# Banded attention scores: the keys' low parts stored on both 64-partition halves

## The chip, the core and the metric

The kernel runs on one core of a Trainium2 chip. The metric is the device time of one execution in microseconds (us); the median of several runs counts. The engines are named as in the profile: PE is TensorE (matmul), PEld its weight loads, DVE is VectorE, ACT is ScalarE, POOL is GpSimd, SP is SyncE, which issues the DMAs.

## What is computed

Two layers of a transformer trunk over 1024 tokens of width 1024, in float32. Each layer has a mixer, a cross attention to 256 memory tokens and an MLP. The mixer of layer 0 is a recurrent one; that of layer 1, the only place that the change touches, is attention in a sliding window of 128 keys, with 16 query heads of size 64, 4 key heads and a sink per head. Cut to what matters:

```
q = rotary(q.reshape(B, S, SW_HEADS, SW_HD), positions).reshape(B, S, SW_KV_HEADS, SW_GROUP, SW_HD)
k = rotary(k.reshape(B, S, SW_KV_HEADS, SW_HD), positions)
...
    def block(j):
        ...
        s = jnp.einsum('blkgd,bckd->bkglc', qb, kb).astype(jnp.float32) * scale
        s = jnp.where(valid, s, -jnp.inf)
        m = jnp.maximum(jnp.max(s, axis=-1), sink)
        p = jnp.exp(s - m[..., None])
        den = jnp.sum(p, axis=-1) + jnp.exp(sink - m)
        ob = jnp.einsum('bkglc,bckd->blkgd', p, vb.astype(jnp.float32))
        ob = ob / jnp.moveaxis(den, -1, 1)[..., None]
```

Block j has 128 queries; its keys are those of blocks j - 1 and j, and `valid` keeps the last 128 positions of each query. The sum of `s` runs over the 64 features d of a head.

## The kernel before, in words

**Precision.** Every float32 operand x of a matmul is split into a high part h, rounded to the type that PE multiplies fast, and a low part l = x - h. A product x y is made of h h, h l and l h. In most of the kernel these are three matmuls (`mm3`). In the banded attention the three are folded into two, since a head has only 64 features and PE has 128 rows: the stationary operand `qT` holds a query head's high part on one 64-partition half and its low part on the other, and the keys' high part stands on both halves (`K1`). One matmul over 128 rows then gives (q_high + q_low) k_high. The second matmul gives q_high k_low and takes 64 rows only: `ql[hp]`, the half with the query's high part, against `K2`, in which the low parts of two key heads share a tile, one on each half.

**Tiling.** `mixer1` is called for each half of the tokens (512, four tiles of 128). It first makes keys and values for the four tiles (`proj_tok`, `rope`, `keys`, `stage`), then the queries in two column blocks `s`; for each tile and pair of key heads `queries` splits the rotated queries and `attend` runs for one token tile `t` and one key head `g`. So `attend` runs 4 x 4 = 16 times in each half. In `stage2` each run multiplies 4 query heads with the keys: for `t` > 0 the two blocks of keys are one operand of 256 columns, so 8 matmuls; for the first tile of half 0 it is 8 matmuls of 128 columns, and for the first tile of half 1, whose earlier keys are kept in `kprev`, 16 of 128 columns. In all 192 matmuls of 256 columns and 96 of 128, half of them over 64 rows, in strict alternation with those over 128.

**After the scores** ACT copies one half of the columns to `p`, DVE merges the other half in (`copy_predicated`), DVE takes the maximum, ACT the exponentials, POOL normalises and masks, PE transposes `p` back (`stage3`) and multiplies with the values (`stage4`).

**Order.** Matmuls are issued in the order of emission (`ordered("pe", ...)`). Emission follows a nominal clock: `pe(us)` advances it, `defer(d, fn)` puts a step off by d nominal microseconds, and the constants `Q1` to `Q3`, `A1` to `A3`, `B1` to `B3` say how far. A score stage counts as 1.0 us on it (`pe(1.0)`). The order on DVE, ACT and POOL follows from the same emission through a scheduler; each of these engines works strictly in its order. The tiles of the mixer come from one pool of 35 buffers (`X`).

Of the kernel before, what the change touches and what calls it, by code (L numbers as in the profile page):

```python
# [59 lines left out]
def trunk(ctx: ExitStack, tc, a, out, stop=99):  # L60
# [6 lines left out]
    def ordered(key, ins):  # L67
        """Issue the instructions of one key in the order of emission."""
        if key in last_of:
            tc.add_manual_dep(  # L70
                ins.ins,
                last_of[key],
                mybir.DependencyInfo(mybir.DependencyClass.NoSync, mybir.DependencyReason.DATA),
                reason="order",
            )
        last_of[key] = ins.ins.name
        return ins
# [28 lines left out]
    # The order of emission: work that waits for other engines is put off by some  # L106
    # microseconds of the tensor engine's work; a filler's pieces go in between.
# [18 lines left out]
    # The filler: groups (load, start, parts); loads run one group ahead of the starts,  # L126
    # and these one group ahead of the parts.
# [9 lines left out]
    def fill(begin=True):  # L137
        """One piece of the filler; False when there is none left."""
        while True:
            if begin and len(parts) < 2 + 1 and (todo or loaded):  # L140
                load_ahead(1)
                g = loaded.pop(0)
                c = g[1]()
                parts.extend(g[2])
                load_ahead(la[0])
                if c == 0.0:
                    continue
            elif parts:
                c = parts.pop(0)()
            else:  # L150
                return False
            clock[0] += c
            due()
            return True
# [13 lines left out]
    def in_steps(gen, n, d):  # L168
        """Emit n instructions of gen every d microseconds."""

        def step():
            for _ in range(n):
                if next(gen, step) is step:
                    return
            defer(d, step)

        step()
# [36 lines left out]
    def table(**kw):  # L214
        """An activation with a table function, in the order of emission."""
        return ordered("table", act(**kw))
# [4 lines left out]
    # ---------------------------------------------------------------- constants  # L221
# [17 lines left out]
    def columns(rows, n):  # L239
        """[n rows of P] -> [P, n]."""  # L240
        ps = T()
        transpose(out=ps[:, 0:n], in_=rows[0:n], identity=ident[0:n, 0:n])
        t = cp.tile([P, n], F32, name=nm("col"))
        vec.tensor_copy(t, ps[:, 0:n])
        return t
# [6 lines left out]
    # ---------------------------------------------------------------- helpers  # L252
    def rsqrt(ss, n):
        """1 / sqrt(sum(ss) / D + EPS) of [P, 2] partial sums (D a power of 4)."""
        v = small(4, n)
        x, xh, y, t = v[:, 0:1], v[:, 1:2], v[:, 2:3], v[:, 3:4]
        vec.tensor_scalar(out=x, in0=ss[:, 0:1], scalar1=ss[:, 1:2], scalar2=D * EPS, op0=ALU.add, op1=ALU.add)  # L257
        vec.tensor_scalar(  # L258
            out=y.bitcast(I32), in0=x.bitcast(I32), scalar1=-0.5, scalar2=float(0x5F3759DF + (5 << 23)), op0=ALU.mult, op1=ALU.add
        )  # L260
        vec.tensor_scalar(out=xh, in0=x, scalar1=-0.5 / D, scalar2=None, op0=ALU.mult)  # L261
        for _ in range(3):
            vec.scalar_tensor_tensor(out=t, in0=y, scalar=y, in1=xh, op0=ALU.mult, op1=ALU.mult)  # L263
            vec.scalar_tensor_tensor(out=y, in0=t, scalar=1.5, in1=y, op0=ALU.add, op1=ALU.mult)  # L264
        return y
# [6 lines left out]
    def square_sum(x, out):  # L272
        """out = sum of the squares of x [P, HALF]; the squares themselves go to a PSUM bank."""
        act(out=T("junk"), in_=x, func=AF.Square, accum_out=out)  # L274
# [12 lines left out]
    def transposed(un, dsts):  # L287
        """un^T times each gain, as (h, l) pairs; dsts: (gain columns, h [P, 8, 128], l)."""
# [16 lines left out]
    def pre_norm(h, g, u, t, delay, where=None):  # L305
        """where: normalised rows go to X tiles, replace h, or go to a tile like h."""
# [20 lines left out]
    def ready(u):  # L327
        """Emit what the four token tiles of u still need."""
        while left[id(u)]:
            clock[0] = max(clock[0], pend[0][0])  # L330
            due()

    def post_half(y, dst, g, ss, n, eng):
        """dst = y * g and the sum of the squares of y, for columns n of a token tile."""
# [4 lines left out]
    def post_norm(yg, ss, hsrc, hdst, i):  # L339
        """h = h + yg * rstd; returns the new h."""  # L340
# [34 lines left out]
    def tick(k, K, us):  # L375
        """After k of K tiles' products; every FINE of them, others may come in between."""
# [10 lines left out]
    def proj_T(w, u, n=HALF, ps=None):  # L387
        """[128 features, tokens] = w^T u^T; w: [P, 2, 8, 128], u = (h, l)."""
# [6 lines left out]
    def proj_tok(ws, u, t, ps=None):  # L395
        """[128 tokens of tile t, n] = u w; ws: list of [P, 2, kn, n]."""
# [10 lines left out]
    def w_out(W, q, n, paired):  # L407
        """Rows of K tiles 2 q and 2 q + 1; paired: tile 4 p + i has heads 8 p + i and 8 p + 4 + i."""
# [7 lines left out]
    def out_proj(W, y, g, hsrc, hdst, half, after=None, lhs=None, paired=False, early=()):  # L416
        """Token-major product with W [1024, 1024], post-norm and residual, per token tile."""
# [32 lines left out]
    def proj_lhs(ws, lhs, ks=None, ps=None):  # L450
        """lhs: list over k of (h, l) stationary [P, 128] blocks; ks: the part of k to add to ps."""
# [12 lines left out]
    # ------------------------------------------------- memory products (cross attention)  # L464
# [6 lines left out]
    def memory_T(l, eng):  # L471
        """(mem * g_mem[l])^T as (h, l)."""
# [19 lines left out]
    def memory_scale():  # L492
        """1 / rms of the memory's tokens, along the free axis on all partitions."""
# [19 lines left out]
    def memory_kv(l, c):  # L513
        """Rows c and c + 1 (of P) of kvd[l] = (rms_norm(mem, g_mem[l]) W_kv)^T."""
# [52 lines left out]
    # log1p(e) / e on [0, 1], a polynomial exact to 7e-10  # L567
# [5 lines left out]
    def log1p_steps(e, q):  # L573
        """q = log1p(e), one instruction per step."""
# [12 lines left out]
    # softplus(-lambda) = max(-lambda, 0) + log1p(exp(-|lambda|)); cs = -4 softplus = log_a / 2 at r = 1  # L587
# [19 lines left out]
    def memory_products(l):  # L607
        """memv[l][(h, m), n] = v W_o, per head, as groups of pieces."""
# [32 lines left out]
    def cross(l, half, u, hsrc, hdst, after, mid):  # L641
# [4 lines left out]
        def scores(h, q, kT, i):  # L646
            """Head h of the tokens of tiles 2 i and 2 i + 1."""
# [52 lines left out]
    def mlp(l, u, hsrc, hdst, after):  # L700
        """u: per half (h, l)."""
# [4 lines left out]
        for c in range(8):  # L706
# [39 lines left out]
            else:  # L746
# [4 lines left out]
                if after is not None:  # L751
                    # the last tiles column by column, so that half of the weights' space is free early
# [10 lines left out]
    # ---------------------------------------------------------------- layer 0 mixer  # L763
# [15 lines left out]
    def gate_weights():  # L779
# [3 lines left out]
        for k, w in enumerate(wg):  # L783
            vec.tensor_copy(w, onez[:, 1:2, None].broadcast_to([P, 4, 100]))
            # columns 0: input gate, 32: forget gate; 64 and 96: their low parts
# [108 lines left out]
    def mlstm(half, u, h, vs, gs, yh, yl):  # L894
# [121 lines left out]
        def stage4(hh):  # L1016
# [3 lines left out]
            # sigmoid(o) = (1 + tanh(o / 2)) / 2, the half being in 1 / den  # L1020
# [21 lines left out]
    def rglru(u, n, rg):  # L1042
# [37 lines left out]
        # gelu (tanh form): y * sigmoid(2 sqrt(2 / pi) (y + 0.044715 y^3))  # L1080
# [15 lines left out]
    def rglru_scan(rg, yh, yl):  # L1096
        # with t = tanh(log_a / 2), sqrt(1 - a^2) = (1 + a) sqrt(-t)
# [42 lines left out]
    # ---------------------------------------------------------------- layer 1 mixer  # L1140
# [56 lines left out]
    def rope(ps, nh, t, n):  # L1197
        """ps [P, nh * 64] (PSUM) -> rotated [P, nh, 64]."""
# [24 lines left out]
    def mixer1(half, u, hsrc, hdst, before_out):  # L1223
        K1 = [X(dt=F32R, n="K1") for _ in range(4)]
        K2 = [X(dt=F32R, n="K2") for _ in range(2)]
# [3 lines left out]
        for t in range(TPH):  # L1229
# [14 lines left out]
            def keys(t=t, kr=kr):  # L1244
                sh, sl = X((P, 4, 2, 64), F32R, "ksh"), X((P, 4, 64), F32, "ksl")
                act(out=sh, in_=kr[:, :, None, :].broadcast_to([P, 4, 2, 64]), func=AF.Copy)
                vec.tensor_tensor(out=sl, in0=kr, in1=f(sh[:, :, 0]), op=ALU.subtract)
                defer(K2D, lambda: stage(t, sh, sl))

            def stage(t, sh, sl):  # L1250
# [4 lines left out]
                for h in range(2):  # L1255
                    transpose(out=pl[:, h * P : (h + 1) * P], in_=sl[:, 2 * h : 2 * h + 2].rearrange("p e d -> p (e d)"), identity=ident)
                for h in range(4):
                    act(out=K1[h][:, c], in_=pk[:, h * P : (h + 1) * P], func=AF.Copy)
                for h in range(2):
                    vec.tensor_copy(K2[h][:, c], pl[:, h * P : (h + 1) * P])  # L1260
                if half == 0 and t == TPH - 1:
                    prev["K1"], prev["K2"] = X((P, 4, P), F32R, "kprev"), X((P, 2, P), F32R, "kprev")
                    act(out=prev["K1"], in_=pk.rearrange("p (h t) -> p h t", h=4), func=AF.Copy)
                    vec.tensor_copy(prev["K2"], pl[:, 0:256].rearrange("p (h t) -> p h t", h=2))
# [29 lines left out]
    def attend(half, t, g, qst, K1, K2, V, dV, last, yh, yl):  # L1294
# [15 lines left out]
        def stage2():  # L1310
            st = small(24, "at", 4)
            mx, m, nmx, den, es, rc = (st[:, 4 * i : 4 * i + 4] for i in range(6))
            hp = slice(64 * (g % 2), 64 * (g % 2) + 64)
            parts = [(K1[g][:, cur], K2[g // 2][hp, cur])]
            if t:
                both = slice((t - 1) * P, (t + 1) * P)
                parts = [(K1[g][:, both], K2[g // 2][hp, both])]
            elif not first:
                parts.insert(0, (last["K1"][:, g], last["K2"][hp, g // 2]))
            w = P if t == 0 else 2 * P  # L1320
            # Each key position modulo 128 is in a query's window once, in this block or in the one before.
            for j in range(2):
                ps = T()
                p3 = ps.rearrange("p (h c) -> p h c", h=2)
                for h in range(2):
                    ql = qT[:, 2 * j + h]
                    for i, (k1, k2) in enumerate(parts):
# [3 lines left out]
                        mm(o, lhsT=ql[hp], rhs=k2, start=False, stop=True)  # L1331
# [49 lines left out]
        def stage4():  # L1381
            po = T("po")
            # The columns of V are (high, low) of an even head and (low, high) of an odd one.
# [13 lines left out]
    # ---------------------------------------------------------------- the trunk  # L1397
# [89 lines left out]
def _constants():  # L1487
    """Identity, band masks, rotary frequencies, head selectors: all of them follow from the shapes alone."""
# [34 lines left out]
```

## Time and profile before

| | us |
|---|---|
| median of 3 runs | 2969.77 |
| lowest, highest run | 2967.55, 2976.97 |
| span of the profiled execution | 2974.9 |
| PE busy in it | 2872.5 (97%) |
| DVE, ACT, POOL busy | 1610.6, 1142.2, 548.6 |
| attention of half 0, of half 1 (stretches read below) | 1600 to 1751, 1836 to 1990 |

The profile gives no time of the profiled execution other than its span, which lies between the lowest and the highest run and 5.1 us above the median. PE is busy nearly throughout, but the profile's busy time of a matmul reaches from its start to a modelled end, so a busy PE need not be a PE at its peak. What tells the rate is the distance from one matmul's start to the next one's. The profile's chain of the work that ended last covers only the last steps of the program here and says nothing of the attention. The granted clock of PE is shown as a share of full speed; its two levels are 1.2 and 2.4 GHz, 0.50 and 1.00 in the rows.

### The profile page before, as it was taken

The numbers are of one execution on the slowest core, as the hardware profiler recorded it, in microseconds if no ns is written. First come the engines' busy times: TensorE is split into PE (matmuls) and PEld (weight loads), VectorE is DVE, ScalarE is ACT, GpSimd is POOL, SyncE is SP. The second block draws the span as 40 slices with busy tenths as digits, with TensorE's granted clock in tenths as the row PEclk, the third lists the DMA queues.
The fourth block names the chain that finished last, engine by engine and source line by source line (L and its number), as shares of the span: only waits on it lengthen the run. The fifth ranks groups of instructions, "written<-read, shape, count | busy, mean of one in ns | idle before, by whom it ended". The sixth has DMA issues, their size and how long they took to land. (4 is left out here: it accounts for less than half of the span.)

```text
span 2974.9 us, 35481 instructions
## 1 busy us (share of the span) xinstructions
PE 2872.5 (97%) x13502; PEld 2360.3 (79%) x13502; DVE 1610.6 (54%) x3152; ACT 1142.2 (38%) x2271; POOL 548.6 (18%) x442
## 2 busy tenths in 40 slices
PE   8999999899999999999989899989999999999998
PEld 8988778788788888888867678767878888888886
DVE  7776586656562333333377866675756133333336
ACT  5555454455443111222144654554554211122112
POOL 1341242512110000000042442550211000000003
PEclk9999999899999999999999899789999999999999
DMA  8633533244321111111133154024423111111113
GB/s 251 190 90 108 183 113 85 91 143 157 103 95 43 51 49 43 57 43 50 50 128 117 60 157 142 8 79 143 158 94 108 50 43 56 44 43 57 43 50 113
DMA packets 265754, 274.29 MB, mean 92 GB/s; under 512 B 11784, under 2 KB 200688, under 8 KB 265584
## 3 DMA queue, kind: packets, MB, share of 16 engines
q1 hardware_dynamic: 265584, 272.03, 29.3%
q8 instruction: 106, 1.74, 0.2%
q14 instruction: 64, 0.52, 0.1%
HBM read 234.24 MB, written 37.75 MB: 91 GB/s over the span
## 5 line engine op out<-in xcount | busy, mean ns | idle before, releaser
L82 PE MATMUL g<-uh,w 128*128 128x512 f32 x3200 | 1008.9, 391 | 1.5 <-ACT uh L299 1.5
L82 PEld LDWEIGHTS g<-uh,w 128*128 128x128 f32 x3200 | 601.7, 188 | 126.0 <-ACT uh L299 2.4
L82 PE MATMUL g<-w,hh 128*128 128x512 f32 x2048 | 641.9, 394 | 1.4 <-DVE acc L738 1.4
L212 DVE TENSOR_TENSOR w<-wr,w 128x1024 fp32r<-128x1024 f32 x344 | 437.1, 1273 | 355.6 <-ACT w L211 354.5
L82 PE MATMUL g<-ul,w 128*128 128x512 f32 x1600 | 623.8, 390 | 1.7 <-POOL ul L300 1.7
L211 ACT ACTIVATE w<-wr 128x1024 fp32r<-128x1024 f32 x344 | 362.7, 1056 | 580.3 <-PE g L82 505.4
L82 PEld LDWEIGHTS g<-w,hh 128*128 128x128 f32 x2048 | 384.2, 188 | 92.2 <-DVE acc L738 1.8
L82 PE MATMUL g<-w,hl 128*128 128x512 f32 x1024 | 403.7, 394 | 0.0
L82 PEld LDWEIGHTS g<-ul,w 128*128 128x128 f32 x1600 | 301.0, 188 | 62.8 <-POOL ul L300 2.3
L738 DVE TENSOR_TENSOR acc<-g,acc 128x512 f32<-128x512 f32 x224 | 154.3, 689 | 299.8 <-PE g L82 298.5
L718 DVE TENSOR_TENSOR rl<-g,rl 128x512 f32<-128x512 f32 x128 | 88.5, 692 | 379.1 <-ACT rl L717 379.1
L337 POOL TENSOR_TENSOR acc<-acc,gain 128x512 f32<-128x512 f32 x32 | 44.5, 1398 | 1335.6 <-ACT junk L274 1335.6
L717 ACT ACTIVATE rl<-g 128x512 f32<-128x512 f32 x128 | 76.4, 597 | 427.7 <-PE g L82 425.1
L82 PEld LDWEIGHTS g<-w,hl 128*128 128x128 f32 x1024 | 192.3, 188 | 45.6
L300 POOL TENSOR_TENSOR ul<-ut,uh 128x512 fp32r<-128x512 f32 x96 | 137.8, 1456 | 404.0 <-ACT uh L299 404.0
L82 PE MATMUL g<-w,uh 128*128 128x512 f32 (+1 forms) x640 | 176.8, 366 | 10.7 <-DVE w L212 4.8
L82 PE MATMUL g<-w,pTh 128*128 128x512 f32 x512 | 161.1, 396 | 0.5 <-ACT pTh L211 0.5
L82 PEld LDWEIGHTS g<-w,uh 128*128 128x128 f32 x640 | 113.1, 196 | 27.1 <-DVE w L212 5.1
L82 PE MATMUL g<-w,ul 128*128 128x512 f32 (+1 forms) x320 | 114.2, 357 | 0.0
L212 DVE TENSOR_TENSOR hl<-rl,hh 128x512 fp32r<-128x512 f32 x128 | 89.3, 697 | 44.3 <-ACT hh L211 44.3
L82 PEld LDWEIGHTS g<-w,pTh 128*128 128x128 f32 x512 | 94.8, 188 | 21.7 <-ACT pTh L211 1.0
L82 PE MATMUL g<-w,pTl 128*128 128x512 f32 x256 | 101.2, 395 | 0.0
(326 smaller groups left out, 3878.5 us busy)
## 6 DMA issues: line engine op xcount, KB each, us to landing
wr<-in_w_ff SPq DMA_DIRECT2D x128, 512.0 KB, 3.9
h<-h SPq DMA_DIRECT2D x100, 512.0 KB, 3.6
wr<-in_ev_w_in SPq DMA_DIRECT2D x48, 512.0 KB, 3.7
wr<-in_w_xkv SPq DMA_DIRECT2D x32, 512.0 KB, 5.8
wr<-in_w_xq SPq DMA_DIRECT2D x32, 512.0 KB, 4.1
wr<-memv SPq DMA_DIRECT2D x32, 512.0 KB, 3.8
wr<-in_od_w_qkv SPq DMA_DIRECT2D x24, 512.0 KB, 4.4
h<-in_x SPq DMA_DIRECT2D x16, 512.0 KB, 4.4
```

The lines of the kernel that those rows point to most:

```text
L82: ins = nc.tensor.matmul(*ar, **kw)
L211: act(out=h, in_=src, func=AF.Copy)
L212: (eng or vec).tensor_tensor(out=l, in0=src, in1=f(h), op=ALU.subtract)
L300: pool.tensor_tensor(out=ul[:, q], in0=t, in1=f(uh[:, q]), op=ALU.subtract)
L337: eng.tensor_tensor(out=dst, in0=y, in1=g[:, c], op=ALU.mult)
L717: act(out=r, in_=ps, func=AF.Relu)
L718: vec.tensor_tensor(out=r, in0=ps, in1=r, op=ALU.mult)
L738: vec.tensor_tensor(out=acc[t][n], in0=ps, in1=acc[t][n], op=ALU.add)
```

## The change

The low parts of the keys are now stored like the high ones, on both 64-partition halves, one tile for each key head: `K2` has four tiles instead of two, `ksl` is 512 columns wide instead of 256, there are four transposes of it for a token tile instead of two and four copies out of PSUM instead of two, and `kprev` for the low parts is twice as wide. The second score matmul then takes the whole of `qT`, 128 rows: it also adds q_low k_low, which the kernel before left out.

```diff
-        K2 = [X(dt=F32R, n="K2") for _ in range(2)]
+        K2 = [X(dt=F32R, n="K2") for _ in range(4)]
...
-                sh, sl = X((P, 4, 2, 64), F32R, "ksh"), X((P, 4, 64), F32, "ksl")
-                act(out=sh, in_=kr[:, :, None, :].broadcast_to([P, 4, 2, 64]), func=AF.Copy)
-                vec.tensor_tensor(out=sl, in0=kr, in1=f(sh[:, :, 0]), op=ALU.subtract)
+                sh, sl = X((P, 4, 2, 64), F32R, "ksh"), X((P, 4, 2, 64), F32, "ksl")
+                k2 = kr[:, :, None, :].broadcast_to([P, 4, 2, 64])
+                act(out=sh, in_=k2, func=AF.Copy)
+                vec.tensor_tensor(out=sl, in0=k2, in1=f(sh), op=ALU.subtract)
...
-                for h in range(2):
-                    transpose(out=pl[:, h * P : (h + 1) * P], in_=sl[:, 2 * h : 2 * h + 2].rearrange("p e d -> p (e d)"), identity=ident)
+                for h in range(4):
+                    transpose(out=pl[:, h * P : (h + 1) * P], in_=sl[:, h].rearrange("p e d -> p (e d)"), identity=ident)
...
-                for h in range(2):
+                for h in range(4):
                     vec.tensor_copy(K2[h][:, c], pl[:, h * P : (h + 1) * P])
...
-                    prev["K1"], prev["K2"] = X((P, 4, P), F32R, "kprev"), X((P, 2, P), F32R, "kprev")
+                    prev["K1"], prev["K2"] = X((P, 4, P), F32R, "kprev"), X((P, 4, P), F32R, "kprev")
...
-                    vec.tensor_copy(prev["K2"], pl[:, 0:256].rearrange("p (h t) -> p h t", h=2))
+                    vec.tensor_copy(prev["K2"], pl.rearrange("p (h t) -> p h t", h=4))
...
-            hp = slice(64 * (g % 2), 64 * (g % 2) + 64)
-            parts = [(K1[g][:, cur], K2[g // 2][hp, cur])]
+            parts = [(K1[g][:, cur], K2[g][:, cur])]
...
-                parts = [(K1[g][:, both], K2[g // 2][hp, both])]
+                parts = [(K1[g][:, both], K2[g][:, both])]
...
-                parts.insert(0, (last["K1"][:, g], last["K2"][hp, g // 2]))
+                parts.insert(0, (last["K1"][:, g], last["K2"][:, g]))
...
-                        mm(o, lhsT=ql[hp], rhs=k2, start=False, stop=True)
+                        mm(o, lhsT=ql, rhs=k2, start=False, stop=True)
```

On PE the order of all matmuls stays, with 16 more transposes. Where the keys of the first token tile of half 0 are transposed (`ksh` and `ksl` are the keys' high and low parts, `g` a running projection), before:

```order
L82 MATMUL g_12788<-w_12693,ul_12192 128x512
L86 MATMUL t_12801<-cst,ksh_12756 128x128 x4
L86 MATMUL t_12802<-cst,ksl_12757 128x128 x2
L82 MATMUL g_12788<-w_12698,uh_12191 128x512 x2
L82 MATMUL g_12788<-w_12698,ul_12192 128x512
```

and with the change:

```order
L82 MATMUL g_12790<-w_12695,ul_12192 128x512
L86 MATMUL t_12803<-cst,ksh_12758 128x128 x4
L86 MATMUL t_12804<-cst,ksl_12759 128x128 x4
L82 MATMUL g_12790<-w_12700,uh_12191 128x512 x2
L82 MATMUL g_12790<-w_12700,ul_12192 128x512
```

Two more transposes stand at the same place; the score matmuls stand where they stood, each `t<-K,qT` pair with the same outputs.

On DVE the copies of the low keys double, and in each half one split of a weight (`w<-wr`, for the query projection that follows) is put ahead of the copies instead of behind them. At the keys of the second token tile of half 0, before:

```order
L1209 TENSOR_TENSOR rq_12841<-g_12788,cos_sin_5581 128x4x32
L1260 CAST K_12684<-t_12861 128x128
L1260 CAST K_12685<-t_12861 128x128
L212 TENSOR_TENSOR w_12915<-wr_12913,w_12915 128x1024
L1247 TENSOR_TENSOR ksl_12875<-kr_12840,ksh_12874 128x256
L212 TENSOR_TENSOR w_12920<-wr_12918,w_12920 128x1024
```

and with the change:

```order
L1209 TENSOR_TENSOR rq_12847<-g_12790,cos_sin_5581 128x4x32
L212 TENSOR_TENSOR w_12925<-wr_12923,w_12925 128x1024
L1261 CAST K_12684<-t_12867 128x128
L1261 CAST K_12685<-t_12867 128x128
L1261 CAST K_12686<-t_12867 128x128
L1261 CAST K_12687<-t_12867 128x128
L1248 TENSOR_TENSOR ksl_12885<-kr_12846,ksh_12884 128x512
L212 TENSOR_TENSOR w_12930<-wr_12928,w_12930 128x1024
```

There are two copies more, `ksl` is twice as wide, and the split of the weight has moved from behind the copies to ahead of them. The next split of a weight likewise comes to stand ahead of the rotary product of the fourth tile's keys. The same holds once in half 1; POOL and SP keep their order, and on ACT two neighbours change places in each half.

## Rows read from the trace of the kernel before

**Rows 1.** The page: busy time of each engine; granted clock in 40 slices.

```profile
PE 2872.5 (97%) x13502; PEld 2360.3 (79%) x13502; DVE 1610.6 (54%) x3152; ACT 1142.2 (38%) x2271; POOL 548.6 (18%) x442
PEclk9999999899999999999999899789999999999999
```

**Rows 2.** Busy time by stretch: length, engines (count), clock, DMA share, GB/s.

```profile
1600.00:1751.00 151.00, 134.68 (x578) 98.25 (x577) 123.62 (x274) 104.60 (x301) 73.58 (x62) 0.93 0.32 99
1836.00:1990.00 154.00, 139.97 (x536) 102.57 (x534) 113.78 (x262) 89.13 (x275) 79.25 (x66) 0.81 0.14 42
```

**Rows 3.** The same of instructions with `qT` alone: PE, PEld, ACT, clock.

```profile
1600.00:1751.00 151.00, 41.16 (x128) 25.30 (x128) 9.20 (x16) 0.93 0.32 99
1836.00:1990.00 154.00, 55.08 (x160) 34.34 (x160) 9.41 (x16) 0.81 0.14 42
```

**Rows 4.** Timeline of PE, one score stage of 256 columns: start, us, instruction.

```profile
1630.63 2.58 PE L82 MATMUL t<-K,qT 128*128 128x256 f32 x8
1633.13 0.72 PE L82 MATMUL g<-w,uh 128*128 128x512 f32 x2
```

**Rows 5.** Timeline of PE, cross attention's scores: first of 24, and what follows.

```profile
2000.16 0.28 PE L82 MATMUL sc<-kvh,qh 128*128 128x256 f32 x1
...
2002.99 0.40 PE L82 MATMUL g<-uh,w 128*128 128x512 f32 x1
```

**Rows 6.** Timeline of PE, one score stage of 128 columns and what follows.

```profile
1616.62 2.01 PE L82 MATMUL t<-K,qT 128*128 128x128 f32 x8
1618.56 0.66 PE L86 MATMUL t<-cst,qst 128*128 128x128 f32 x4
```

**Rows 7.** Timeline of PE, layer 0: 2 over 4 rows, 4 transposes, 12 products.

```profile
264.71 0.49 PE L82 MATMUL t<-Mh,nsel 4*128 4x512 f32 x1
...
265.36 0.66 PE L86 MATMUL t<-cst,k 128*128 128x128 f32 x4
265.77 0.31 PE L82 MATMUL t<-qh,kh 128*128 128x128 f32 x1
...
267.14 0.44 PE L82 MATMUL g<-uh,w 128*128 128x512 f32 x1
```

**Rows 8.** Weight loads of the cross attention's scores: count, ns min/median/max, first and last.

```profile
L82 PEld LDWEIGHTS sc<-kvh,qh x128: 186/188/193, 578.2 to 2210.2; 128*128 128x128 f32 x128
```

**Rows 9.** Busy time in parts of the two stretches, columns as in rows 2.

```profile
1600.00:1645.00 45.00, 45.00 (x204) 33.13 (x202) 32.66 (x84) 30.20 (x103) 14.34 (x16) 1.00 0.15 42
...
1700.00:1751.00 51.00, 42.87 (x199) 31.40 (x199) 47.34 (x101) 41.51 (x103) 34.76 (x24) 0.99 0.67 210
1836.00:1890.00 54.00, 53.37 (x226) 38.87 (x225) 37.90 (x90) 31.48 (x106) 21.78 (x22) 0.94 0.11 30
```

**Rows 10.** Who waited for whom, 1600 to 1980: us in total, times, longest.

```profile
ACT p L1333 <- PE t L82: 43.2, 44, 2.0
...
PE t L82 <- ACT qT L1306: 9.5, 8, 3.9
```

**Rows 11.** DVE by line, 1570 to 1840: count, busy us, mean ns, idle before.

```profile
L1260 DVE CAST K<-t 128x128 fp32r<-128x128 f32 x16 | 3.9, 284 | 0.7 <-PE t L86 0.7
L1247 DVE TENSOR_TENSOR ksl<-kr,ksh 128x256 f32<-128x256 f32 x8 | 3.4, 426 | 6.2 <-ACT ksh L1246 6.2
```

**Rows 12.** Busy time where the keys are made, columns as in rows 2.

```profile
1560.00:1600.00 40.00, 35.04 (x159) 28.56 (x158) 30.59 (x78) 15.01 (x37) 13.15 (x17) 0.96 0.51 180
1800.00:1836.00 36.00, 36.00 (x173) 29.92 (x172) 22.84 (x59) 13.95 (x35) 11.23 (x16) 1.00 0.50 168
```

**Rows 13.** Busy time around a fall of the clock in half 1, columns as before.

```profile
1848.70:1855.50 6.80, 6.80 (x30) 4.63 (x29) 6.43 (x12) 4.07 (x10) 3.01 (x3) 1.00 0.36 106
1855.60:1862.30 6.70, 6.70 (x19) 4.85 (x19) 3.37 (x13) 3.32 (x13) 1.31 (x2) 0.50 0.31 85
```

**Rows 14.** Timeline of PE: a wait before a score stage (idle time and releaser in brackets).

```profile
1661.29 0.48 PE L82 MATMUL t<-K,qT 128*128 128x128 f32 x1 [3.89 <-ACT qT L1306]
```

**Rows 15.** Busy time in the stretch behind that wait, columns as in rows 2.

```profile
1661.00:1674.00 13.00, 12.71 (x29) 8.70 (x30) 6.80 (x16) 4.73 (x15) 2.85 (x3) 0.50 0.00 0
```

## The prediction

> **What bounds the kernel now.** I read the page first. PE is busy 97% of the span, so time that leaves PE's stream tends to leave the kernel, unless another engine is close behind [rows 1]. The page's clock shows full speed nearly everywhere; its drops lie in the attention among other places. Next the stretches: attention takes 1600 to 1751 us for half 0 and 1836 to 1990 us for half 1, 305 us together, at a granted clock of 0.93 and 0.81 [rows 2]. DVE is busy 123.62 of 151 us there and 113.78 of 154: it is the engine that would be late next.
>
> Then PE alone. The 288 score matmuls are 41.16 + 55.08 = 96.24 us of PE's busy time [rows 3], a third of what PE does there. Their rate is what is odd. A stage of 8 matmuls of 256 columns runs from 1630.63 to the next start at 1633.13 without a wait: 2.50 us, 0.3125 us each [rows 4]. Cross attention has matmuls of the same 256 columns and the same type, all over 128 rows: 24 of them take 2000.16 to 2002.99, 2.83 us, 0.118 us each [rows 5]. With 128 columns the banded scores take 1616.62 to 1618.56, 1.94 us for 8 or 0.2425 us each [rows 6]; layer 0 has 12 full-row products of that width in 265.77 to 267.14, 1.37 us or 0.114 us each [rows 7]. The one thing that sets the slow ones apart is that every second one uses 64 rows. Layer 0 has another place where the rows change: two products over 4 rows of 512 columns start at 264.71 and are over at 265.36, 0.325 us each [rows 7], and there too the step into and out of the narrow form costs more than full-row products do.
>
> **The change, part by part.**
>
> *Removed: the alternation.* All score products then use 128 rows. I take for each the distance of its full-row counterpart. 192 x (0.3125 - 0.118) = 37.3 us and 96 x (0.2425 - 0.114) = 12.3 us, together 49.7 us of PE's stream. Half 0 has 96 wide and 32 narrow ones: 18.7 + 4.1 = 22.8 us. Half 1 has 96 and 64: 18.7 + 8.2 = 26.9 us. This prices all of them at full clock. The upper end comes from the busy time as it was, slow clock included: 192 x 0.118 + 96 x 0.114 = 33.6 us is what they need at full clock, so 96.2 - 33.6 = 62.6 us would go if they all ran so.
>
> *Added on PE: 16 transposes of 128 columns.* The four in layer 0 start at 265.36 and the next product at 265.77, 0.10 us each [rows 7]: 16 x 0.10 = 1.6 us. They stand between projections, in a stretch where PE is busy 36.00 of 36 us [rows 12], so I count them whole. Net on PE: 48 to 61 us.
>
> *Added on DVE: 16 copies and a doubled subtraction.* 16 x 0.284 = 4.5 us, and 8 subtractions of twice the width, at most another 0.426 each, 3.4 us [rows 11]; the wider `kprev` is one more piece of that size. Together 8 us, 4 in each half, while the keys are made. DVE is busy 30.59 of 40 and 22.84 of 36 us there, and PE has no wait in the second of these [rows 12]; the queries' projections that follow are long PE work and need nothing of these copies. I count nothing. Without that cover it would be those 8 us. A split of a weight that goes ahead of the copies is due earlier than they are and costs nothing for the same reason. Two more buffers of 35 are held through the attention; fewer free buffers cannot gain, and no wait on one is among the large ones in the trace; I take nothing, and as the other bound one wait like ACT's longest, 2.0 us [rows 10].
>
> *What is next late.* ACT waits 43.2 us for PE's scores, in 44 waits [rows 10], and the copies behind them on ACT, and the merges on DVE that wait for ACT, get that back. That speaks for the gain going through. Against it stands DVE's load. The best use that DVE reaches in a long stretch here is 47.34 of 51 us, 93% [rows 9]. At that use half 0 cannot be shorter than 123.62 / 0.928 = 133.2 us, which allows 17.8 us of the 22.8. Half 1 could come down to 113.78 / 0.928 = 122.6 us, which allows 31.4, more than PE's 26.9. So I take 17.8 + 26.9 - 1.6 = 43 us. The clock I leave as it was. In the profile's own span that is 2974.9 - 43 = 2932 us; the median lies 5.1 us below that span, so 2927 us.
>
> **A rule that speaks against it.** The weight load of a full-row product takes 0.188 us [rows 8], longer than the 0.118 us between two such products [rows 5]: loads run beside products that use the same rows. The Trainium skill, "TensorE: Matmul & The Clock Gate", part 3 ("Packing small matmuls", under "The mechanism"), says that a load overlaps products in flight only when the row groups differ. By that rule full-row pairs would stay serial and the sum would be near zero; the trace does not bear it out.
>
> **The rivals.**
>
> *DVE and ACT take back more.* Only where PE has no idle time is its gain sure: 1600 to 1645 (45.00 of 45 us busy) and 1836 to 1890 (53.37 of 54) [rows 9]. Whole stages in these are 11 of 8 wide products and, in sets of 8, 6 of narrow ones (two stages of 8, two of 16): 88 x 0.1945 + 48 x 0.1285 = 23.3 us. If the rest vanishes into waits for `qT` and for the masks, the gain is 10 to 33 us, around 22: 2937 to 2960. For it: DVE at 93% in 1700 to 1751. Against it: that stretch waits on ACT, which itself waits for scores.
>
> *The clock comes back as well.* At 1855.6 the clock falls to 0.50, the 1.2 GHz level, and stays there to 1862.3; in the 6.8 us before it PE was busy throughout, 19 of its 30 products being scores in alternation [rows 13]. So it was not a wait of PE that preceded this fall. Denser scores could spare some falls; then PE nears the 61 us, and DVE's limit at 93% is 17.8 + 31.4 = 49 us, at 100% 27 + 40 = 67. Gain 50 to 68: 2902 to 2920. The Trainium skill, "TensorE: Matmul & The Clock Gate", section "A second HAM failure mode: psum-queue depth-cycling", describes such falls from short idle pieces between groups of products; no row here separates that from other causes.
>
> *No effect.* The distance of 0.3125 us comes from something else, as serial loads would give: 0.188 + 0.118 = 0.306 us. Then only the 1.6 us are added: 2965 to 2975. Against it: rows 5 and 7.
>
> *Slower, by the clock.* PE gets to the places where it waits earlier and waits longer. Before 1661.29 it waited 3.89 us for `qT` [rows 14], and in the stretch behind that the clock was 0.50 [rows 15]. PE's work other than scores is 274.65 - 96.24 = 178 us, at full clock some 155 (mean clock 0.87), with the new scores 188; idle time is now 30 us. If 60% of it ran at half clock: 188 x 1.6 + 30 = 331 us against 305, 26 us slower, 2996. It decides from (305 - 30) / 188 = 1.46, that is when 46% of the work runs slowly; today the lost clock of 0.07 and 0.19 means 14% and 38% of the time. I see no reason for so much more of it.
>
> **How the numbers follow.** Chances: forecast, gain of 33 to 50 us (2920 to 2937), 0.50; DVE and ACT take more (2937 to 2960), 0.25; clock comes back (2902 to 2920), 0.15; no effect, 0.05; slower, 0.05. The forecast's time is 2927. A range of 2905 to 2955 leaves out the last two and the edges of the second and third, some 0.16 together. A difference of 0.3%, 9 us, is about what runs of this kernel can tell from none: faster by more than that 0.90, within it 0.05, slower 0.05.
>
> **What would show it.** In the changed kernel's timeline a score stage of 8 wide products should take about 1.0 us instead of 2.50, and all shapes read 128x128 rows; the 288 products' PE time should fall from 96 us to some 40. ACT's wait for scores should fall well below 43 us. DVE should reach 90% or more in both stretches, and PE's idle time there should grow from 30 us; if it does not grow, the gain is at the high end. If a stage stays at 2.5 us, the row change was not the cause. If stages are at 1.0 us and the time is the same, waits of PE for `qT`, the masks or the clock have taken it all.

## The result, and the profile after

The changed kernel takes 2943.65 us (median; 2938.32 to 2945.52), the kernel before 2973.37 (the three runs of before and a fourth of 2985.71): a ratio of 0.9891, interval 0.9869 to 0.9912, or 29.7 us less. The forecast was 2927 in a range of 2905 to 2955. The range holds; the forecast's own value is 16.7 us too low, of which 3.6 is the fourth run's effect on the median it was counted from (2969.77), and the time lies where the first rival put it (2937 to 2960). So the cause was right and some 13 of the 43 us did not arrive. The profiled executions exaggerate the gain: they have spans of 2974.9 and 2936.5, 38.4 us apart, since of the kernel before one of the longer runs was profiled and of the changed one the shortest.

**The score stage did what was forecast.** PE's timeline in the changed kernel, a stage of 8 wide and one of 8 narrow products, each with what follows it (start, us, instruction):

```profile
1629.93 1.10 PE L82 MATMUL t<-K,qT 128*128 128x256 f32 x8
1630.86 0.64 PE L82 MATMUL g<-w,uh 128*128 128x512 f32 x2
...
1616.77 1.00 PE L82 MATMUL t<-K,qT 128*128 128x128 f32 x8
1617.61 0.63 PE L86 MATMUL t<-cst,qst 128*128 128x128 f32 x4
```

0.93 us instead of the 2.50 of [rows 4], 0.84 instead of the 1.94 of [rows 6]. The busy time of all instructions with `qT` in the two stretches (length, PE, PEld, ACT, clock, DMA share, GB/s) answers to [rows 3]:

```profile
1601.70:1739.50 137.80, 20.14 (x128) 18.04 (x128) 9.19 (x16) 0.91 0.34 109
1825.50:1951.60 126.10, 24.21 (x160) 21.94 (x160) 9.46 (x16) 0.91 0.17 51
```

Together 44.35 us instead of 96.24; the prediction said some 40. All engines in the same stretches (PE, PEld, DVE, ACT, POOL, clock, DMA share, GB/s), answering to [rows 2]:

```profile
1601.70:1739.50 137.80, 114.09 (x578) 92.17 (x577) 123.37 (x274) 103.16 (x301) 73.38 (x62) 0.91 0.34 109
1825.50:1951.60 126.10, 99.12 (x536) 83.13 (x534) 112.33 (x261) 87.44 (x274) 78.82 (x66) 0.91 0.17 51
```

PE's idle time has grown from 30.3 to 23.7 + 27.0 = 50.7 us, DVE's work is the same in shorter stretches. The waits show the exchange (us in total, times, longest):

```profile
PEld t L82 <- ACT qT L1307: 24.8, 15, 3.5
ACT p L1349 <- DVE at L1342: 23.8, 14, 4.6
...
PE t L82 <- ACT qT L1307: 19.5, 13, 3.1
...
ACT p L1333 <- PE t L82: 4.8, 10, 0.9
```

ACT's wait for scores, 43.2 us in [rows 10], is down to 4.8 us. In its place ACT waits for DVE's maxima (23.8), and PE for `qT` 19.5 us instead of 9.5.

**Where the time went.** To compare runs I measure each half from its first score product to the last product of its outputs (`po`), a cut with the same instructions in every kernel. In these rows half 0 stands first, half 1 second. Before:

```profile
1605.70:1750.80 145.10, 128.78 (x551) 93.35 (x549) 121.42 (x269) 103.28 (x298) 71.89 (x60) 0.93 0.33 103
1840.10:1999.90 159.80, 145.49 (x560) 107.23 (x559) 116.99 (x265) 91.32 (x277) 81.57 (x68) 0.82 0.15 44
```

After:

```profile
1607.40:1739.20 131.80, 108.14 (x550) 87.20 (x548) 121.13 (x269) 101.84 (x298) 71.70 (x60) 0.91 0.35 113
1829.50:1961.50 132.00, 105.02 (x561) 87.88 (x560) 117.52 (x265) 89.88 (x277) 81.12 (x68) 0.91 0.18 53
```

Half 0 is 13.3 us shorter: 20.6 less PE work, 7.4 more idle time. Half 1 is 27.8 us shorter: 40.5 less PE work, 12.7 more idle time. Score products account for 30.9 of these 40.5 ([rows 3] against the row above), so 9.6 is other work that ran at a higher clock. Ahead of the scores the changed kernel takes 1.7 us more in half 0 and 0.9 more between the halves, where 1.6 was counted for the keys of both.

Half 0 gained only in its first 76 us, which became 62. Its last 69 us, in three pieces, before:

```profile
1682.00:1702.00 20.00, 16.65 (x61) 11.70 (x60) 18.59 (x41) 14.23 (x39) 7.35 (x7) 0.83 0.42 142
1702.00:1723.50 21.50, 18.03 (x87) 13.11 (x85) 20.69 (x63) 19.89 (x52) 7.04 (x7) 1.00 0.47 152
1723.50:1751.00 27.50, 22.84 (x106) 16.68 (x106) 24.65 (x35) 19.99 (x47) 26.00 (x17) 0.98 0.82 255
```

and the same pieces after:

```profile
1669.40:1690.60 21.20, 16.12 (x66) 12.44 (x65) 19.52 (x41) 15.05 (x40) 7.63 (x8) 0.76 0.41 140
1690.60:1712.00 21.40, 15.28 (x83) 12.82 (x82) 20.58 (x63) 19.21 (x51) 6.94 (x7) 0.90 0.49 166
1712.00:1739.50 27.50, 22.66 (x103) 16.84 (x102) 24.73 (x35) 19.97 (x47) 25.98 (x17) 0.93 0.78 239
```

The lengths are the same although PE has less to do. In the middle piece DVE is busy 96% of the time, before as after; in the last one POOL is at 95%, 26.00 and 25.98 of 27.50 us. PE's timeline at the end of half 0 in the changed kernel shows the last outputs, each behind a masked block (`pTm`) of POOL's:

```profile
1733.32 0.50 PE L82 MATMUL po<-pTm,dv 128*128 128x512 f32 x1 [0.61 <-POOL pTm L1377]
...
1736.78 0.50 PE L82 MATMUL po<-pTm,dv 128*128 128x512 f32 x1 [1.71 <-POOL pTm L1377]
```

In the kernel before, the counterparts of these two waited 0.54 and 1.74 us.

### The profile page after: what moved, and what is told of

Read it like the earlier page. It is cut to its first block, busy times and chain, and to the rows that moved or that the text cites. A ratio compares the mean times of both kernels' runs of the same rounds, so it can differ in the third digit from the quotient of the medians.

```text
span 2936.5 us, 35526 instructions
## 1 busy us (share of the span) xinstructions
PE 2816.4 (96%) x13518; PEld 2340.3 (80%) x13518; DVE 1617.2 (55%) x3168; ACT 1139.1 (39%) x2271; POOL 548.8 (19%) x442
## 3 DMA queue, kind: packets, MB, share of 16 engines
q8 instruction: 106, 1.74, 0.2%
## 5 line engine op out<-in xcount | busy, mean ns | idle before, releaser
L300 POOL TENSOR_TENSOR ul<-ut,uh 128x512 fp32r<-128x512 f32 x96 | 136.3, 1440 | 403.0 <-ACT uh L299 401.9
L82 PEld LDWEIGHTS g<-w,uh 128*128 128x128 f32 x640 | 111.9, 194 | 25.7 <-DVE w L212 5.1
```

Of the source, the lines that this page charges most:

```text
L82: ins = nc.tensor.matmul(*ar, **kw)
L300: pool.tensor_tensor(out=ul[:, q], in0=t, in1=f(uh[:, q]), op=ALU.subtract)
```

## The experiments

Each ratio is to the kernel before, run on the same chip beside the experiment.

### Is it the change of rows?

Storage as in the changed kernel, products as before (`hp` picks the 64 rows again):

```diff
-                        mm(o, lhsT=ql, rhs=k2, start=False, stop=True)
+                        mm(o, lhsT=ql[hp], rhs=k2, start=False, stop=True)
```

> The changed kernel's storage (low keys on both halves, 16 more transposes, 16 more copies), but the second score product again over 64 rows. Theory, that the alternation of 64 and 128 rows is what costs: a wide score stage takes 2.50 us again, and the time is that of the kernel before plus 0 to 4 us, ratio 1.000 to 1.0015. Rival, that the storage or the other use of buffers brought part of the gain: the time lies 5 us or more below the kernel before, with score stages still at 2.50 us.

2980.43 us, ratio 1.0022 (1.0011 to 1.0032), some 6 us more, where the theory had 0 to 4. A stage takes 2.50 us again, 1632.01 to 1634.51 (a merged line of the timeline carries the form of its first product; four of these eight are over 64 rows):

```profile
1632.01 2.57 PE L82 MATMUL t<-K,qT 128*128 128x256 f32 x8
1634.51 0.72 PE L82 MATMUL g<-w,uh 128*128 128x512 f32 x2
```

The gain belongs to the products, and the wider storage costs a little. In the profiled run, 3.6 us longer, the first score product comes 1.4 us later; half 0 is 0.8 and half 1 1.9 us longer, at a clock of 0.91 and 0.81.

The other way round: the kernel before with its 64-row products, issued so that two of one kind stand next to each other (K1 K1, K2 K2 K2 K2, K1 K1 in a stage):

```diff
-                for h in range(2):
-                    ql = qT[:, 2 * j + h]
...
+            for h in range(2):
+                for i, (k1, k2) in enumerate(parts):
+                    for n, low in enumerate((flip, not flip)):
+                        for j in range(2):
+                            ql, o = qT[:, 2 * j + h], p3s[j][:, h, c : c + w]
...
+                    flip = not flip
```

> The kernel before, 64-row products kept, but ordered so that a wide stage is two products over 128 rows, four over 64, two over 128: two changes of rows instead of eight. Theory, a price for each change: 6 x 0.118 + 2 x 0.31 = 1.33 us for a wide stage, three quarters of the price gone, 37 us of PE's stream, and of that some 23 to 30 us in the time, ratio 0.990 to 0.992. Rival, that a product over 64 rows is slow by itself: its distance stays 0.31 us in the middle of the four, a stage takes 1.7 to 2.0 us, and the gain is under 17 us.

2949.82 us, ratio 0.9925 (0.991 to 0.994): 25 us less, without one more copy or transpose. A stage in its timeline:

```profile
1637.26 1.60 PE L82 MATMUL t<-K,qT 128*128 128x256 f32 x8
1638.69 0.60 PE L86 MATMUL t<-cst,qst 128*128 128x128 f32 x4
```

It takes 1.43 us. Products over 64 rows are not slow: in the stage that starts at 1628.86 the distances from start to start are 0.12, 0.21, 0.22, 0.12, 0.12, 0.21, 0.22 and 0.12 us, 1.33 us together, as the theory said. Where a product has its like on both sides, 64 rows take the 0.118 of 128 rows; each of the two changes adds about 0.195 us, spread over two distances. Eight times 0.118 and eight changes of 0.195 make the 2.50 us of [rows 4]. The stage shown takes 0.1 us more, as does the one at 1626.72: both come right behind transposes, and the first distance is 0.22 instead of 0.12; no run asks why. At 128 columns a change costs less: the alternating products of [rows 6] settle at 0.255 us each, full-row ones of the changed kernel at 0.112, so about 0.14. The Trainium skill, "TensorEngine Tiling (Array Packing)", "Key Properties", says that a change of the tiling mode drains TensorE and gives no price. In this case's trace a change of rows costs time, 0.195 us at 256 columns and 0.14 at 128; whether that is a drain no run here shows.

### Who holds the rest of half 0 back?

The changed kernel again, beside the next one:

> The changed kernel once more, on the same chip as the other three, for comparison with them: ratio 0.987 to 0.991.

2943.58 us, ratio 0.9905 (0.989 to 0.992).

The changed kernel, and then the kernel before, without one addition on DVE in half 0 (16 instructions of 0.69 us; left out is the product with the low part of the values; the text of the second run calls it, wrongly, the sum of the two query groups' outputs):

```diff
-            vec.tensor_tensor(out=yl[r, k, cur], in0=p3[o], in1=f(yl[r, k, cur]), op=ALU.add)
+            if half:
+                vec.tensor_tensor(out=yl[r, k, cur], in0=p3[o], in1=f(yl[r, k, cur]), op=ALU.add)
```

> The changed kernel without one DVE instruction of each attention step of half 0 (the addition of the values' low part to the output's low part, 16 x 0.69 = 11 us); that term is left out of the computation in half 0. Theory, that DVE bounds the last third of half 0's attention: half 0 ends 5 to 11 us earlier than in the changed kernel, ratio 0.002 to 0.004 below it. Rival, that the waits there come from the chain of the filler's weights (buffer, DMA, ACT) or from latencies: under 2 us.

2938.57 us, ratio 0.9886 (0.9869 to 0.9903), 5.0 less than the changed kernel beside it; half 0 takes 127.5 us (131.8 and 132.3 in the two profiles with the addition). That is 4.3 to 4.8 us, just under the theory's 5 to 11 and clear of the rival's 2.

> The kernel before, without one addition on DVE in half 0 (the sum of the two query groups' outputs, 11 us of DVE's time; half 1 keeps it). Theory: the last part of half 0 was bound by DVE already before the change (57 busy us of PE, 63.4 of DVE in 68.5 us), so that part has little to gain from lighter products; then half 0 ends 4 to 7 us earlier here too, about as much as the same edit gave in the changed kernel, and the ratio is near 0.998. Rival: with the slow products PE was the bound there, and DVE became it only with the change; then the end of half 0 moves by 2 us or less and the ratio is 0.9995 or more.

2969.03 us, ratio 0.9988 (0.9965 to 1.0011): no verdict, the runs spread over 23 us. Half 0 takes 144.0 us instead of 145.1, which by the letter is the rival's side. But the row shows why this run decides nothing:

```profile
1609.40:1753.40 144.00, 132.36 (x551) 95.11 (x549) 111.18 (x255) 103.41 (x298) 70.71 (x60) 0.91 0.33 104
```

PE is idle 11.6 us instead of 16.3, so taking DVE's work away did save 4.7 us of waits; PE's busy time rose by 3.6, at a clock of 0.91 instead of 0.93. So I turned the question round: DVE's subtraction for the output's low part done twice in half 0, 11 us more, in the kernel before and in the changed one:

```diff
             split(yh[r, k, cur], yl[r, k, cur], p3[r])
+            if half == 0:
+                vec.tensor_tensor(out=yl[r, k, cur], in0=p3[r], in1=f(yh[r, k, cur]), op=ALU.subtract)
```

> The kernel before with the subtraction that gives the low part of an attention output done twice in half 0: 16 more instructions of 0.69 us, 11 us of DVE's time. Theory (DVE bound half 0's last part only after the change): before, PE's slow products left DVE some room, so half 0 ends 3 to 6 us later, about half of what is added. Rival 1 (DVE bound that part before as well, and the lighter products could bring nothing there): as in the changed kernel with the same addition, 6 to 10 us later. Rival 2 (DVE bounds nothing here): 2 us or less.

2981.4 us, ratio 1.0021 (1.001 to 1.0033).

> The changed kernel with the same doubled subtraction in half 0, 11 us of DVE's time more. Theory: DVE sets the pace of half 0 from 1640 on; most of the 11 us arrives, half 0 ends 6 to 10 us later and the kernel takes 5 to 10 us more than the changed one. Rival (fixed delays of the chain, not DVE's load): 3 us or less.

2947.68 us, ratio 0.9906 (0.9879 to 0.9934), 4 us above the changed kernel's median. Half 0 of the first and of the second:

```profile
1605.90:1759.80 153.90, 133.89 (x551) 97.57 (x549) 129.44 (x281) 104.02 (x298) 69.99 (x60) 0.89 0.28 91
...
1606.10:1743.10 137.00, 108.27 (x551) 87.73 (x549) 128.01 (x281) 102.17 (x298) 70.09 (x60) 0.91 0.33 103
```

Half 0 of the kernel before gets 8.8 us longer (rival 1: 6 to 10), that of the changed one 5 (the theory said 6 to 10, so a little less arrives). But 5.1 of the 8.8 are PE's busy time, at a clock of 0.89 instead of 0.93. With waits alone, to leave out the clock, the 11 us more cost 3.7 us of PE's idle time before (20.0 against 16.3) and 5.0 after (28.7 against 23.7); the 11 less gave back 4.7 and 3.2. That is about 0.3 to 0.45 us of wait for each us of DVE's work, on either side of the change. My theory that DVE became the bound only with the change is not borne out: by their waits the two kernels are about equally sensitive.

Where in half 0 the 11 us less count is a question of its own. The last part of half 0, from the same instruction of DVE (a `pTl`, at 1682.44 us before and 1670.60 after) to the last output, of the kernel before, the changed one, and then both without the addition:

```profile
1682.40:1750.80 68.40, 56.91 (x249) 41.07 (x248) 63.36 (x135) 53.72 (x135) 40.39 (x29) 0.94 0.60 191
...
1670.60:1739.20 68.60, 52.61 (x241) 40.82 (x239) 63.36 (x135) 53.03 (x133) 40.35 (x29) 0.87 0.59 189
...
1681.60:1753.40 71.80, 61.98 (x250) 43.71 (x249) 57.29 (x125) 54.01 (x136) 36.91 (x28) 0.88 0.56 183
...
1665.80:1734.70 68.90, 54.09 (x246) 40.43 (x244) 57.26 (x126) 53.45 (x136) 39.80 (x29) 0.88 0.60 191
```

What goes before takes 76.7, 63.2, 72.2 and 58.6 us. So leaving out the addition gave 4.5 us ahead of the last part, and in it nothing, although DVE has 6 us less to do there (in the kernel before at a lower clock, in the changed one at the same); the theory had the place wrong. More work on DVE does lengthen the last part, by 8.0 us before and 3.9 after. The last 20 us of it have a bound that can be read: POOL does 13 instructions without a pause, with the addition and without it (changed kernel):

```profile
1719.20:1739.20 20.00, 15.74 (x69) 11.21 (x67) 17.47 (x19) 13.06 (x28) 19.96 (x13) 0.98 0.80 240
...
1714.70:1734.70 20.00, 16.18 (x66) 10.76 (x65) 13.89 (x16) 13.05 (x28) 19.92 (x13) 0.92 0.80 248
```

In the kernel before it is the same 20.0 us, 1730.8 to 1750.8. No run made POOL's work lighter; the next one makes it heavier. What sets the 48 us ahead of that is not shown: DVE is busy 94% of them in the changed kernel, but its load alone is not the limit.

Then half of a further DVE load, the splits of the filler's weights (products of the memory, issued in the attention's gaps), moved to POOL in the changed kernel:

```diff
-                split(w[:, 0], w[:, 1], st["raw"])
+                split(w[:, 0], w[:, 1], st["raw"], pool if l and n else vec)
```

> The changed kernel with the subtraction that gives the low part of a weight (for the products of the memory in layer 1, which fill the attention's gaps) on POOL instead of DVE in every second group, about 10 us of DVE's time less in the attention. Theory: DVE is the bound of half 0's last part, so taking half of these 10 us there gives 2 to 5 us over the changed kernel. Rival: POOL takes longer for each (2.6 us and more), it stands in the way of POOL's masks and normalisation, and the filler's products come later: the same as the changed kernel or up to 5 us slower.

2949.9 us, ratio 0.9917 (0.9898 to 0.9937): 6 us more than the changed kernel. What the rival named happened, and cost a little more than its 5 us. POOL's timeline near the end of half 0 shows the split standing in front of the masks:

```profile
1733.54 3.38 POOL L212 TENSOR_TENSOR w<-wr,w 128x1024 fp32r<-128x1024 f32 x1
...
1739.13 1.29 POOL L1377 TENSOR_TENSOR pTm<-pTh,mask_prevT 128x512 fp32r<-128x512 f32 x1
```

Half 0 takes 138.6 us instead of 131.8, and PE's idle time in it rises from 23.7 to 30.9.

### Are the new waits for qT what is left?

The scores emitted 2 nominal us later behind the transposes of their queries, in the changed kernel (twice) and in the kernel before, and 4 us later in the changed one:

```diff
-A1, A2, A3 = 1.5, 6.0, 6.0
+A1, A2, A3 = 3.5, 6.0, 6.0
```

> The changed kernel with the scores emitted 2 nominal us later behind the transposes of their queries (A1 is 3.5, was 1.5), so that other products of PE stand in between. Theory: in the changed kernel PE arrives earlier at the scores and waits for qT (19.5 us for products, 24.8 for their weight loads, the same 13 to 15 times); that is what half 1 lost of its gain; with more work in between the waits fall by half and the kernel is 3 to 10 us faster than the changed one (ratio to the kernel before 0.986 to 0.990, beside 0.9905 for the changed one). Rival: DVE and ACT set the pace, and the waits move to the next product that needs them: within 2 us of the changed kernel.

2940.76 us, ratio 0.9882 (0.9857 to 0.9908). The waits halve, as expected:

```profile
PEld t L82 <- ACT qT L1307: 11.5, 5, 6.8
...
PE t L82 <- ACT qT L1307: 9.8, 4, 6.6
```

> The changed kernel with the scores emitted 2 nominal us later (A1 is 3.5) once more, with more rounds: its median was 2940.8, that of the changed kernel 2943.7 and 2943.6 in two looks, and the intervals overlap. If the 3 us are real, the median is again 2939 to 2942 and the ratio to the kernel before 0.987 to 0.989; if they are not, it is 2942 to 2946 and 0.989 to 0.991.

2942.62 us, ratio 0.9876 (0.9856 to 0.9895), between the two answers: the median is that of no gain, the ratio that of a gain. By the medians 1 to 3 us are gained; the intervals overlap with those of the changed kernel, and it isn't settled that any are.

> The kernel before with the same later emission of the scores (A1 is 3.5). Theory: before the change PE waited for qT 9.5 us, 8 times, half as much as in the changed kernel; so the same edit gives half as much or nothing here, 0 to 4 us, ratio 0.9985 to 1.000. Rival: the nominal delay is simply badly chosen in both, and gives as much here as in the changed kernel.

2979.51 us, ratio 1.0011 (0.9997 to 1.0026): nothing gained, at best.

> The changed kernel with the scores emitted 4 nominal us later behind the transposes of their queries (A1 is 5.5; 1.5 in the changed kernel, 3.5 in the run before this). At 3.5 the waits for qT had halved (29 to 9.8 + 11.5 us for products and loads, from 19.5 + 24.8) and some 3 us were gained. Theory: the rest of these waits goes as well, another 1 to 4 us. Rival: the chain behind the scores is now the longer one, and later scores make the later steps late: no gain over 3.5, or a loss of up to 5 us.

(The "29" in this text is a slip; the two waits were 19.5 and 24.8.) 2944.55 us, ratio 0.9893 (0.987 to 0.9915). The waits for `qT` at the scores are all but gone, 1.1 and 1.5 us, and the time is that of the changed kernel. Nor is PE's idle time smaller: 25.7 + 25.6 us in the halves of the first of these kernels, 25.2 + 25.8 in the last, 23.7 + 27.0 without the edit. So the wait for `qT` was only where PE met the pace of the chain through ACT, DVE and POOL; without that meeting point it waits as long elsewhere.

## Why the prediction was right, and where not

**The cause: right.** The distance of 0.3125 us came from the alternation of rows. Undoing the products alone brings it back, grouping them takes most of it away.

**The size on PE: right.** 49.7 us at full clock, 62.6 at the clocks of the profile; measured 96.24 - 44.35 = 51.9 us, with the clock at 0.91 in both halves.

**The additions: small, as said, but not resolved.** 1.6 us were counted; between these two profiles the way to the scores became 2.6 us longer. That is within what the same code varies: the first score product comes at 1605.7 to 1609.4 us in four profiles with the old storage and at 1606.1 to 1609.0 in six with the new. The 8 us of DVE's copies, counted as hidden, do not appear there. The storage alone cost 4 us in the profile and 6 in the median, more than the 1.6; most of it appears in the attention, where PE issues the same products and is 1.4 and 1.6 us longer busy with them at a slightly lower clock. I did not find its cause.

**Half 0, the term that was mis-sized: 17.8 us taken, 13.2 measured in the same stretch.** The step that failed is the cap, "at that use half 0 cannot be shorter than 133.2 us". The 151 us that it was set against became 137.8, with DVE at 123.37 of them, 90% instead of 93%; and they were not one stretch with one limit. In the last 68 us, where a quarter of half 0's score products lie, the lighter products brought nothing (68.4 and 68.6 us). POOL holds the last 20 us; what holds the 48 before them stays open, since neither lighter products nor a lighter DVE shortened them. The page showed POOL at 18% of the span and [rows 2] at 49% of half 0, so I left it out of the sum; it needed a cut as fine as the pieces above. [rows 9] had DVE at 93% from 1700 on, and I used that row for a rate instead of reading it as a place where PE's gain may end.

**Half 1: 26.9 us taken, 27.8 in the two profiles, but by another route.** The forecast left the clock alone and counted no new waits. In fact waits took 12.7 us and a higher clock gave some 10 to 14. And the agreement is partly luck. Other runs have the same instructions in half 1. In the two kernels that differ from before only in half 0 it takes

```profile
1841.80:1993.50 151.70, 137.85 (x560) 102.74 (x559) 120.61 (x265) 91.67 (x277) 80.64 (x68) 0.87 0.15 46
...
1846.30:1999.60 153.30, 137.97 (x560) 101.88 (x559) 118.87 (x265) 91.67 (x277) 80.78 (x68) 0.87 0.16 45
```

at a clock of 0.87, against 159.8 at 0.82. The run with the changed storage and the old products has the same score products and is at the low clock again:

```profile
1842.30:2004.00 161.70, 147.11 (x560) 108.30 (x559) 117.31 (x265) 91.47 (x277) 81.57 (x68) 0.81 0.14 43
```

So the profile I predicted from had caught half 1 at the lower of two clocks, each of which was met twice. The mean of the first three is 154.9 us, of all four 156.6; of the four profiles with the changed half 1 (132.0, 133.5, 136.3, 137.6) it is 134.9. By these means half 1 gains 20 to 22 us. Then the parts make 13.3 + 20 to 22 - 2.6, some 31 to 32 us, beside the 29.7 of the medians. Of the 13 us that did not arrive, 4.6 were too much taken for half 0, 5 to 7 for half 1, and 1 for the keys; with so few profiles this closes only roughly.

**The rivals.** "DVE and ACT take back more" is what happened in its result; it named the waits for the masks, which POOL makes, but not POOL as a bound. "The clock comes back" happened in part, in half 1: there the clock fell to 0.50 seven times before, for some 58 us of the 159.8, and five times after, for some 24 of 132.0. In half 0 it fell three times before and six times after, for some 21 and 24 us. The new waits, 20 us in both halves, used up more than this gave. I did not test what sets the clock off. "Slower, by the clock" did not come: more waits (50.7 us instead of 30.3) went with a higher mean clock in half 1 and a slightly lower one in half 0.

**What would show it.** Stages near 1.0 us: yes. Some 40 us for the 288 products: 44.35. ACT's wait for scores well below 43: 4.8. DVE at 90% or more in both stretches: just missed, 89.5% and 89.1% (123.37 of 137.80, 112.33 of 126.10). PE's idle time above 30: 50.7.

**What stays open.** What the wider storage costs beyond the keys, what holds the 48 us of half 0 ahead of POOL's last 20, and why the clock in half 1 is 0.81 or 0.82 in two runs and 0.87 in two others. Of the versions that compute the whole result none is shown to beat the changed kernel; the later scores may, by 1 to 3 us.

## What to carry to other kernels

Read PE's rate from the distances between starts and compare it with another place of the same shape: behind a busy share of 97% the score products took 96 us of the attention where 44 were enough. Where row counts alternate, make them equal or issue like beside like; here grouping alone gave 25 of the 30 us without any new storage. Before a gain on one engine is summed over a stretch, cut the stretch until each piece has one limit, and look at every engine in every piece: POOL at 49% of half 0 was the bound of its last 20 us. A busy share near 95% names a suspect, not the bound: DVE had it ahead of POOL, and taking work from it there gained nothing. And a profile is one run: where its clock is low, a second profile of the same code tells how much of a stretch is the clock.

## What the hardware showed that was not expected

A product over 64 rows beside its like takes the same 0.118 us as one over 128; only the change costs, about 0.195 us each at 256 columns and 0.14 at 128, spread over the distances on both sides of it. Full-row products of 128 columns in the score stages stand 0.112 us apart once the stage runs (its first distance is shorter, so that eight take 0.84), only little less than the 0.118 of those of 256. And the granted clock of half 1 with the same products was 0.81 or 0.82 in two runs and 0.87 in two others, which moved it by 6 to 10 us, beside a gain of 29.7.
